# Weights by tiles of 128 columns and one matrix of per-channel vectors in a streaming RWKV-7 / S5 / mLSTM layer

## The chip, the cores and the metric

The kernel runs on one core of one Trainium2 chip. The metric is the device time of one execution in microseconds (us). The engines are PE (matmul; PEld is its weight load), DVE (vector), ACT (scalar), POOL (GpSimd) and SP, whose queue issues most DMA transfers; ACT issues the others. All arithmetic is in float32; the large matmuls run on operands split into a high part, rounded to the matmul's own format, and the remainder.

## The reference

One layer is computed for a prompt of 16 + 2048 tokens and for 64 tokens of a running stream, D = 1024:

```python
proj = (x @ p['w_in']).astype(F32)                       # x: normalised input, w_in: 1024 x 11144
rw_cols, rw_gate, s5_u, s5_gate, ml_qk, ml_v, ml_if, ml_o, ml_z, merge = split_cols(proj, IN_SIZES)
y_rw, ... = rwkv7_branch(rw_cols, rw_gate, ...)          # recurrence with 12 heads of 64
y_s5, ... = s5_branch(s5_u, s5_gate, ...)                # diagonal complex recurrence, then a 512 x 512 GLU
y_ml, ... = mlstm_branch(ml_qk, ml_v, ml_if, ml_o, ml_z, ...)   # 4 heads of 192, chunks
gates = jax.nn.sigmoid(merge + p['b_merge']).reshape(x.shape[:2] + (N_BRANCH, D_MODEL))
merged = (gates[..., 0, :] * (y_rw @ p['w_br_rw']) + gates[..., 1, :] * (y_s5 @ p['w_br_s5'])
          + gates[..., 2, :] * (y_ml @ p['w_br_ml']))
out = merged @ p['w_out']
x_new = layer_norm(DN_ALPHA * x.astype(F32) + out, p['ln_g'], p['ln_b'])
```

It returns x_new for both groups and the states that each branch leaves. There are some twenty per-channel vectors (norm gains and biases, shift weights, conv taps, gate biases, initial states).

## The kernel before

**Blocks.** The 2128 tokens are cut into five blocks (`BLOCKS`, 4 to 7 chunks of 64; block 0 also holds the sample and the meta tokens). Block 0 is loaded and normalised by `ln_first` (L205 to L246), later ones by `ln_stage`, one block ahead. The normalised x, channel on the partition, is held as `xh` and `xl`, eight tiles of 128 channels each.

**Projections.** `proj` (L437) makes 128 output columns of x @ w_in: three products (hi x hi, hi x lo, lo x hi) for each of eight k tiles, 24 matmuls at L434. The weight comes from `load_w` (L416). In block 0, `split_w` (L394) reads the 128 columns from `w_in` in two halves of four k tiles. The view of w_in puts the row within a k tile on the partition, so a half of 128 x 4 x 128 floats (256 KB) consists of 512 pieces of 512 B, each 44.6 KB from the next. ACT casts the half to `whi` (L405), POOL subtracts it to `wlo` (L406), and both are stored to `wsp` in DRAM (L411) in rows of 2 KB. Later blocks load `whi` and `wlo` from there (L425), 512 KB of rows of 2 KB for each half. `wraw` has 3 buffers, `whi` and `wlo` 4 each.

**Order.** Generators for the three branches are interleaved in `mix`; the gate pass (L1502) makes the 24 tiles of the merge gates for a block with its own buffers `ghi`, `glo` and PSUM tag `f`. The framework then schedules all instructions per engine with a model of its own, and each engine and queue runs its list in order. Transfers take eight semaphores in turn, so one waits on its queue until the transfer eight places before it has landed.

**Vectors.** `add_rows` (L265) lists 22 vectors as rows of 128 channels, 294 rows in all. `load_rows` (L294) reads them by 24 transfers on SP (L303) into tiles of 128 rows, PE transposes the tiles (L309) and DVE copies them to `PT` (L310), 128 x 294, so that `pcol` gives a column with the channel on the partition. in_g and in_b are loaded ahead of `ln_first`, the others behind it. `derive` (L315) makes scaled copies on DVE.

**Other weights.** `ml_gates` (L838) reads the 8 columns of the mLSTM's i and f gates as pieces of 32 B, in each of the five blocks. `s5_block` reads `s5_w_glu` at L1416 (4 fetches a block). In `merge_pass`, three passes over tokens fetch w_br_rw, w_br_s5 and w_br_ml in `branch_w` (L1571) and w_out at L1665, all through `split_w` in pieces of 512 B; PE works on them at L1565.

Of the kernel before, what the change touches and what calls it, by code (L numbers as in the profile page):

```python
# [19 lines left out]
KD = D // 128  # L20
# [13 lines left out]
O_RW, O_RG, O_S5U, O_S5G, O_MQ, O_MK, O_MV, O_MIF, O_MO, O_MZ, O_MG = (  # L34
    0, 2432, 3200, 3712, 4224, 4992, 5760, 6528, 6536, 7304, 8072)
# [8 lines left out]
RMAX = 448  # L44
# [39 lines left out]
def tile_trunk(ctx: ExitStack, tc: tile.TileContext, I, O, dbg=None, parts=("rw", "s5", "ml", "mg")):  # L84
    nc = tc.nc
    V, S, G, PE = nc.vector, nc.scalar, nc.gpsimd, nc.tensor
# [6 lines left out]
    wp = ctx.enter_context(tc.tile_pool(name="wp", bufs=1))  # L93
# [20 lines left out]
    def psum(shape, tag):  # L114
        return pt(ps, shape, tag, bufs=PSB[tag])
# [7 lines left out]
    ident = pt(cst, (128, 128), "ident")  # L123
# [138 lines left out]
    rows_spec = []
    col = {}

    def add_rows(name, ap2d):  # L265
        n = ap2d.shape[0]
        col[name] = sum(r[1] for r in rows_spec)
        rows_spec.append((name, n, ap2d))

    def vec(name):  # L270
        return I[name][0].rearrange("(n p) -> n p", p=128)

    add_rows("in_g", I["in_ln_g"].rearrange("(n p) -> n p", p=128))
    add_rows("in_b", I["in_ln_b"].rearrange("(n p) -> n p", p=128))
    add_rows("mu", vec("rw_mu"))
    for nm in ("rw_w0", "rw_a0", "rw_kk", "rw_ka", "rw_ln_g", "rw_ln_b"):
        add_rows(nm, vec(nm))
    add_rows("rk", I["rw_rk"][0].rearrange("(n a) d -> n (a d)", a=2))
    add_rows("shift", I["state_rwkv_shift"][0, 0].rearrange("(n p) -> n p", p=128))
    add_rows("s5_d", vec("s5_d"))  # L280
    add_rows("s5_b_glu", vec("s5_b_glu"))
    add_rows("conv_w", I["ml_conv_w"][0].rearrange("j (n p) -> (j n) p", p=128))
    add_rows("conv_b", vec("ml_conv_b"))
    add_rows("conv_s", I["state_mlstm_conv"][0, 0].rearrange("j (n p) -> (j n) p", p=128))
    add_rows("ml_ln_g", vec("ml_ln_g"))
    add_rows("b_merge", vec("b_merge"))
    for nm in ("s5_a_re", "s5_a_im"):
        add_rows(nm, I[nm][0].rearrange("(q a) p -> q (a p)", a=2))
    for nm in ("state_s5_re", "state_s5_im"):
        add_rows(nm, I[nm][0, 0].rearrange("(q a) p -> q (a p)", a=2))  # L290
    NR = sum(r[1] for r in rows_spec)
    PT = pt(cst, (128, NR), "PT")

    def load_rows(lo, hi, tags):  # L294
        r0, r1 = (col[rows_spec[lo][0]], NR if hi == len(rows_spec) else col[rows_spec[hi][0]])
        rt = [pt(rp, (128, RMAX), tags[i])[:, 0:128] for i in range((r1 - r0 + 127) // 128)]
        r = 0
        for name, n, ap in rows_spec[lo:hi]:
            a = 0
            while a < n:  # L300
                ti, off = divmod(r + a, 128)
                m = min(n - a, 128 - off)
                nc.sync.dma_start(rt[ti][off:off + m, :], ap[a:a + m, :])  # L303
                a += m
            r += n
        for i, t in enumerate(rt):
            m = min(128, r1 - r0 - 128 * i)
            p = psum((128, 128), "tr")
            PE.transpose(p[:, :m], t[:m, :], ident[:m, :m])  # L309
            V.tensor_copy(PT[:, r0 + 128 * i:r0 + 128 * i + m], p[:, :m])  # L310

    def pcol(name, j=0, n=1):
        return PT[:, col[name] + j:col[name] + j + n]
# [3 lines left out]
        V.tensor_scalar(t, pcol(src, 0, n), mul, add, ALU.mult, ALU.add)  # L317
        return t

    load_rows(0, 2, ["rk"])  # L320
    ln_first(blocks[0])
    load_rows(2, len(rows_spec), ["kk", "L", "Bc"])

    ones = pt(c1, (128, 128), "ones")
    V.memset(ones, 1.0)
# [60 lines left out]
                e.dma_start(t.bitcast(F32)[:, :b.T], xT_d[b.i][j, :, k, :])  # L386
                cur[nm].append(t)

    w_in = I["w_in"][0].rearrange("(k p) c -> p k c", p=128)

    WBUF = {"w": (3, 4),
            "g": (2, 2)}
# [23 lines left out]
    def load_w(pool, off, first, tag="w"):  # L416
        nh = WBUF[tag][1]
        if first:
            wh, wl = split_w(pool, w_in[:, :, off:off + 128], KD, 128, tag, keep=off)
            return wh, wl  # L420
        hi, lo = [], []
        for k in range(0, KD, 4):
            for j, (nm, out) in enumerate((("hi", hi), ("lo", lo))):
                t = pt(pool, (128, 4, 128), tag + nm, F32R, bufs=nh)
                nc.sync.dma_start(t.bitcast(F32), wsp_d[off][k // 4, j])  # L425
                out += [t[:, m] for m in range(4)]
        return hi, lo
# [410 lines left out]
    def ml_gates(b):  # L838
        T = b.T
        nch = len(b.tiles)  # L840
        raw = pt(wp, (128, KD, 8), "wraw", bufs=WBUF["w"][0])
        nc.sync.dma_start(raw, w_in[:, :, O_MIF:O_MIF + 8])
        wh, wl = [], []
        for k in range(0, KD, 4):
            h = pt(wp, (128, 4, 128), "whi", F32R, bufs=WBUF["w"][1])
# [468 lines left out]
    def s5_block(b, u_d, y_d):  # L1314
# [82 lines left out]
        for i in range(4):  # L1397
# [11 lines left out]
            V.scalar_tensor_tensor(y, a, 1.0, y, ALU.add, ALU.mult)  # L1409
            Gs.append(y)  # L1410
            yield
        wg = I["s5_w_glu"][0].rearrange("(k p) c -> p k c", p=128)
        for i in range(4):
            ch = slice(128 * i, 128 * i + 128)
            raw = pt(wp, (128, 4, 128), "wraw", bufs=WBUF["w"][0])
            nc.sync.dma_start(raw, wg[:, :, ch])  # L1416
            p = psum((128, 512), "d")
            pv = p[:, :T].rearrange("p (s c) -> p s c", s=8)
            for k in range(4):
                PE.matmul(pv, raw[:, k], Gs[k], start=k == 0, stop=k == 3)  # L1420
# [91 lines left out]
    def merge_pass():  # L1512
# [18 lines left out]
        w_br = {k: I["w_br_" + k][0].rearrange("(k p) c -> p k c", p=128) for k in ("rw", "s5", "ml")}  # L1531
        w_out = I["w_out"][0].rearrange("(k p) c -> p k c", p=128)
        nyk = [0]

        def yk(dt):
# [35 lines left out]
        def branch_w(B, bi, d):  # L1571
            nm, yd, kt = BR[bi]
            th = pt(pool["th"], (128, TB), "th2", bufs=2)
            for b, lo, o, m in seg[B]:
                nc.scalar.dma_start(th[:, o:o + m], g_d[b.i][D * bi + 128 * d:D * bi + 128 * d + 128, lo:lo + m])
            return split_w(wp, w_br[nm][:, :, 128 * d:128 * d + 128], kt, 128) + (th,)

        wnext = branch_w(0, 0, 0)
        ynext = []
# [39 lines left out]
        for B, n_ in enumerate(TBS):  # L1619
# [36 lines left out]
            for grp in ([[slice(0, LG)], [slice(LG, n_)]] if last else [hsl]):  # L1656
                for d in range(8):
                    c0, c1_ = grp[0].start, grp[-1].stop
                    xr = [pt(pool["b"], (128, TB), f"xr{j}", bufs=2) for j in range(2)]
                    for j in range(2):  # L1660
                        for b, lo, o, m in seg[B]:
                            a, e = max(o, c0), min(o + m, c1_)
                            if a < e:
                                nc.scalar.dma_start(xr[j][:, a:e], xT_d[b.i][j, :, d, lo + a - o:lo + e - o])
                    wh, wl = split_w(wp, w_out[:, :, 128 * d:128 * d + 128], KD, 128)  # L1665
                    t = oT[d]
                    for sl in grp:
                        p = psum2((128, sl.stop - sl.start), "g")
# [86 lines left out]
```

## Time and profile before

| | |
|---|---|
| median of 3 runs (lowest, highest) | 4103.11 us (4101.01, 4103.15) |
| profiled execution: its own time, its span | 4099.27 us, 4097.5 us |
| busy share of the span | PE 92%, DVE 62%, ACT 30%, POOL 16% |
| DMA | 837 MB in 814882 packets, 204 GB/s; under 512 B 220262, under 2 KB 574798 packets |
| fetches of 256 KB into wraw | w_in 174, w_out 64, w_br 72 (and 48 of 128 KB), s5_w_glu 20 |

A page of the profile divides the span into 40 slices and gives each a digit, the busy share in tenths. The view by windows gives each engine's busy time in chosen stretches, with PE's granted clock and the busy share of the 16 DMA engines. The share adds up the times of packets, so it can pass 100% in a short stretch. The view of waits tells which engine stood still, and what released it; the chain of waits follows the work that ended last back to its start. Idle time of an engine that nothing waits for costs nothing.

### The profile page before, as it was taken

How to read it: one execution, taken by the hardware profiler on the slowest of the kernel's cores; microseconds unless marked ns; L12 is line 12 of the kernel's file. 1: busy time of each engine (PE TensorE's matmuls, PEld its weight loads, DVE VectorE, ACT ScalarE, POOL GpSimd, SP SyncE). 2: the span in 40 equal slices, each digit the busy share in tenths (PEclk: the TensorE clock that was granted, in tenths of full speed). 3: DMA queues.
4: the chain of work that ended last, by engine and by line, in shares of the span. 5: the costliest groups of instructions: out<-in, count | busy, mean ns of one | idle time of the engine just before them, and what ended most of it. 6: DMA issues, size and time to landing. Idle time of an engine off the chain costs nothing.

```text
span 4097.5 us, 77030 instructions
## 1 busy us (share of the span) xinstructions
PE 3785.1 (92%) x27117; PEld 3302.3 (81%) x27117; DVE 2535.4 (62%) x8332; ACT 1210.1 (30%) x2655; POOL 661.6 (16%) x951
## 2 busy tenths in 40 slices
PE   6886778989999899999999999999999998999997
PEld 5775567878888788888778888878888787999997
DVE  6679875455566556656636656665666554357476
ACT  5443333232222232222322322232323232222222
POOL 5442133200010000001000000000000000232335
PEclk9997798999999999999999999999999999999999
DMA  8995479956676766667675666666575556566555
GB/s 250 287 290 172 124 244 271 299 178 188 185 227 200 240 205 188 206 204 216 201 227 170 210 191 211 205 220 205 175 218 184 167 170 182 170 192 196 157 180 166
DMA packets 814882, 837.19 MB, mean 204 GB/s; under 512 B 220262, under 2 KB 574798, under 8 KB 814494
## 3 DMA queue, kind: packets, MB, share of 16 engines
q1 hardware_dynamic: 736606, 758.96, 60.0%
q10 hardware_dynamic: 77888, 73.28, 6.0%
q8 instruction: 215, 3.52, 0.4%
q14 instruction: 173, 1.42, 0.1%
HBM read 635.89 MB, written 198.18 MB: 204 GB/s over the span
## 4 chain that ended last, share of the span: by engine, by line
PE 63%; DMA 15%; DVE 13%; SPq 3%; issue 2%; ACT 2%; POOL 1%; ACTq 0%; DVEq 0%; POOLq 0%
PE d L434 28%; PE f L434 9%; PE z L1565 7%; PE g L1565 4%; DMA wraw<-in_w_in_dram 2%; PE py L728 1%; PE d L1420 1%; PE tr L581 1%; DMA xT<-X 1%; PE tr L699 1%; PE tr L707 1%; DVE Z L620 1%; DVE Ztmp L618 1%; PE o L1009 1%; DMA Uin<-Ud 1%
## 5 line engine op out<-in xcount | busy, mean ns | idle before, releaser
L434 PE MATMUL d<-xh,whi 128*128 128x448 f32 (+1 forms) x2520 | 946.0, 375 | 47.6 <-ACT whi L405 18.3
L434 PE MATMUL d<-xh,wlo 128*128 128x448 f32 (+1 forms) x2520 | 932.8, 370 | 11.1 <-POOL wlo L406 10.8
L434 PE MATMUL d<-xl,whi 128*128 128x448 f32 (+1 forms) x2520 | 928.4, 368 | 0.0
L434 PEld LDWEIGHTS d<-xh,whi 128*128 128x128 f32 x2520 | 485.6, 193 | 106.6 <-ACT whi L405 21.8
L434 PEld LDWEIGHTS d<-xh,wlo 128*128 128x128 f32 x2520 | 485.2, 193 | 60.5 <-POOL wlo L406 16.1
L434 PEld LDWEIGHTS d<-xl,whi 128*128 128x128 f32 x2520 | 485.9, 193 | 39.6 <-issue 7.0
L406 POOL TENSOR_TENSOR wlo<-wraw,whi 128x512 fp32r<-128x512 f32 (+1 forms) x310 | 397.3, 1291 | 566.3 <-ACT whi L405 534.0
L434 PE MATMUL f<-xh,ghi 128*128 128x448 f32 (+1 forms) x912 | 348.1, 382 | 46.9 <-ACT gt L1509 26.9
L434 PE MATMUL f<-xh,glo 128*128 128x448 f32 (+1 forms) x912 | 342.5, 376 | 9.0 <-DMA glo<-wsp 6.5
L434 PE MATMUL f<-xl,ghi 128*128 128x448 f32 (+1 forms) x912 | 335.4, 368 | 0.0
L405 ACT CAST whi<-wraw 128x512 fp32r<-128x512 f32 (+1 forms) x310 | 180.1, 586 | 459.8 <-PE z L1565 95.9
L618 DVE TENSOR_TENSOR Ztmp<-Uin,Z 128x60 f32<-128x60 f32 (+24 forms) x930 | 206.1, 222 | 103.2 <-DMA Uin<-Ud 90.3
L434 PEld LDWEIGHTS f<-xh,ghi 128*128 128x128 f32 x912 | 178.3, 196 | 72.4 <-ACT gt L1509 33.6
L620 DVE TENSOR_TENSOR Z<-Z,Ztmp 128x60 f32<-128x60 f32 (+24 forms) x930 | 211.0, 227 | 13.6
L434 PEld LDWEIGHTS f<-xh,glo 128*128 128x128 f32 x912 | 178.1, 195 | 29.2 <-DMA glo<-wsp 10.8
L1565 PE MATMUL z<-ya,whi 128*128 128x384 f32 (+1 forms) x784 | 191.6, 324 | 0.6 <-DVE th L1637 0.6
L434 PEld LDWEIGHTS f<-xl,ghi 128*128 128x128 f32 x912 | 178.6, 196 | 12.4 <-issue 1.6
L946 DVE SCALAR_TENSOR_TENSOR X<-X,PT 128x448 f32<-128x448 f32 (+1 forms) x180 | 122.4, 680 | 46.3 <-ACT X L944 42.7
L1565 PEld LDWEIGHTS z<-ya,whi 128*128 128x128 f32 x784 | 137.5, 188 | 1.5 <-DVE th L1637 0.6
L1565 PE MATMUL z<-ya,wlo 128*128 128x384 f32 (+1 forms) x384 | 124.3, 324 | 0.0
L1509 ACT ACTIVATE gt<-f,hbm 128x448 f32<-128x448 f32 (+1 forms) x114 | 69.8, 613 | 181.1 <-PE f L434 150.3
L1565 PE MATMUL z<-yb,whi 128*128 128x288 f32 (+1 forms) x512 | 120.7, 318 | 2.0 <-DVE th L1637 1.8
(732 smaller groups left out, 6863.7 us busy)
## 6 DMA issues: line engine op xcount, KB each, us to landing
whi<-wsp SPq DMA_DIRECT2D x504, 256.0 KB
wlo<-wsp SPq DMA_DIRECT2D x504, 256.0 KB
ghi<-wsp SPq DMA_DIRECT2D x192, 256.0 KB
glo<-wsp SPq DMA_DIRECT2D x192, 256.0 KB
wraw<-in_w_in_dram SPq DMA_DIRECT2D x174, 256.0 KB
wsp<-whi SPq DMA_DIRECT2D x126, 256.0 KB
wsp<-wlo SPq DMA_DIRECT2D x126, 256.0 KB
gt<-gt SPq DMA_DIRECT2D x96, 224.0 KB
```

Source lines behind the costliest of these rows:

```text
L405: S.copy(h[:, :n, :M], raw[:, :n, :M])
L406: G.tensor_tensor(l[:, :n, :M], raw[:, :n, :M], h.bitcast(F32)[:, :n, :M], ALU.subtract)
L434: PE.matmul(p, a[k], c, start=i == 0, stop=i == 3 * KD - 1)
L581: i = PE.matmul(p[h][:, c].rearrange("p (j t) -> p j t", j=2), bk[h][:, c0 + c, :], AQ[hs[h], c0 + c], start=True, stop=True)
L618: V.tensor_tensor(t3, Uin[:, j:j + 1, j + 1:32].to_broadcast((128, m, n)), Z[:, 0:m, j:j + 1].to_broadcast((128, m, n)), ALU.mult)
L620: V.tensor_tensor(Z[:, 0:m, j + 1:32], Z[:, 0:m, j + 1:32], t3, ALU.add)
L699: PE.matmul(p[hs[h], c], Tt[hs[h], c0 + c, :], AR[hs[h], c0 + c], start=True, stop=True)
L707: PE.matmul(p[hs[h], c], PX[hs[h], c0 + c, 0, :], AT[hs[h], c0 + c, h, :], start=True, stop=True)
L728: i = PE.matmul(o, a, x, start=start, stop=stop, skip_group_check=True)
L946: V.scalar_tensor_tensor(acc[:, :w], raw[:, j:j + w], pcol("conv_w", 12 * j + ti), acc[:, :w], ALU.mult, ALU.add)
L1509: S.activation(t[:, :T], p[:, :T], AF.Tanh, scale=0.5, bias=hbm[:, j:j + 1])
L1565: PE.matmul(p, a[k], c[:, sl], start=i == 0, stop=i == n - 1)
```

## The change

Before the kernel is built, `kernel` now lays the inputs out anew with `_layout`: w_in as 87 tiles of 128 columns, each with the row within a k tile first, then the k tile, then the column (`w_tiles`), so that a half tile is 128 pieces of 2 KB; the 8 gate columns apart (`w_if`, 256 B for each partition); the other five weights as tiles in the same way; and the 294 rows of vectors as one matrix of 128 x 294 (`pt`). On the core, `PT` is loaded by one transfer, and `add_rows`, `load_rows`, their transposes and copies are gone. What is computed from weights and vectors, and from which buffers, stays the same.

```diff
-    def load_rows(lo, hi, tags):
...
-                nc.sync.dma_start(rt[ti][off:off + m, :], ap[a:a + m, :])
...
-            PE.transpose(p[:, :m], t[:m, :], ident[:m, :m])
-            V.tensor_copy(PT[:, r0 + 128 * i:r0 + 128 * i + m], p[:, :m])
+    nc.sync.dma_start(PT, I["pt"])
...
-    load_rows(0, 2, ["rk"])
     ln_first(blocks[0])
-    load_rows(2, len(rows_spec), ["kk", "L", "Bc"])
...
-    w_in = I["w_in"][0].rearrange("(k p) c -> p k c", p=128)
+    def w_tile(off):
+        return I["w_tiles"][(off if off < O_MIF else off - 8) // 128]
...
-            wh, wl = split_w(pool, w_in[:, :, off:off + 128], KD, 128, tag, keep=off)
+            wh, wl = split_w(pool, w_tile(off), KD, 128, tag, keep=off)
...
-        nc.sync.dma_start(raw, w_in[:, :, O_MIF:O_MIF + 8])
+        nc.sync.dma_start(raw, I["w_if"])
...
-            nc.sync.dma_start(raw, wg[:, :, ch])
+            nc.sync.dma_start(raw, I["s5_w_glu"][i])
...
-            return split_w(wp, w_br[nm][:, :, 128 * d:128 * d + 128], kt, 128) + (th,)
+            return split_w(wp, I["w_br_" + nm][d], kt, 128) + (th,)
...
-                    wh, wl = split_w(wp, w_out[:, :, 128 * d:128 * d + 128], KD, 128)
+                    wh, wl = split_w(wp, I["w_out"][d], KD, 128)
...
+def _tiles(w):
+    k, c = w.shape
+    return w.reshape(k // 128, 128, c // 128, 128).transpose(2, 1, 0, 3)
```

The change moves instructions. On SP's queue, before, the last row loads (`L` and `Bc` are tiles for rows, `bif` and `msam` small vectors of the mLSTM) stand just ahead of the first fetches of w_in:

```order
L303 DMA L_335<-in_s_a_im_dram 16x128
L303 DMA L_335<-in_state_s_re_dram 10x128
L303 DMA Bc_336<-in_state_s_re_dram 6x128
L303 DMA Bc_336<-in_state_s_im_dram 16x128
L823 DMA bif_424<-in_ml_b_if_dram 4x1
L824 DMA bif_424<-in_ml_b_if_dram 4x1
L826 DMA msam_427<-in_state_mlstm_m_dram 4x1
L404 DMA wraw_465<-in_w_in_dram 128x4x128
L404 DMA wraw_473<-in_w_in_dram 128x4x128
```

They are transfers 24 to 33 of the queue. On SP's queue of the changed kernel, from its first transfer on (`va`, `AT` and `X` are the tiles that x is loaded into):

```order
L267 DMA PT_111<-in_pt_dram 128x294
L214 DMA va_115<-in_x_sample_dram 64x1024
L214 DMA AT_121<-in_meta_dram 16x1024
L214 DMA AT_127<-in_x_prompt_dram 128x1024
L214 DMA X_133<-in_x_prompt_dram 128x1024
L779 DMA bif_385<-in_ml_b_if_dram 4x1
L780 DMA bif_385<-in_ml_b_if_dram 4x1
L782 DMA msam_388<-in_state_mlstm_m_dram 4x1
L360 DMA wraw_426<-in_w_tiles_dram 128x512
L360 DMA wraw_434<-in_w_tiles_dram 128x512
```

The first fetch of w_in is now the ninth transfer and was the thirty-second. On ACT, before, the program begins with the scaling of x (L232) and its casts to `xh` (L241), and the first casts of weights (L405) stand among the latter:

```order
L232 ACTIVATE va_120<-va_120,nb_43_160,rs_40_146 64x1024
L232 ACTIVATE AT_126<-AT_126,nb_43_160,rs_40_146 16x1024
L232 ACTIVATE AT_132<-AT_132,nb_43_160,rs_40_146 128x1024
L232 ACTIVATE X_138<-X_138,nb_43_160,rs_40_146 128x1024
L241 ACTIVATE xh_44_162<-d_179,PT_111 128x64
L241 ACTIVATE xh_48_166<-o_196,PT_111 128x64
L241 ACTIVATE xh_44_162<-d_214,PT_111 128x16
L241 ACTIVATE xh_48_166<-o_231,PT_111 128x16
L405 CAST whi_463<-wraw_465 128x512
```

On ACT of the changed kernel (L361 is the cast of weights, L808 and L809 those of the gate columns):

```order
L361 CAST whi_424<-wraw_426 128x512
L361 CAST whi_432<-wraw_434 128x512
L808 CAST whi_484<-wraw_482 128x4x4 x2
L808 CAST whi_494<-wraw_482 128x4x4 x2
L809 CAST wlo_485<-wraw_482 128x4x4 x2
L809 CAST wlo_495<-wraw_482 128x4x4 x2
L232 ACTIVATE va_115<-va_115,nb_41_155,rs_38_141 64x1024
L232 ACTIVATE AT_121<-AT_121,nb_41_155,rs_38_141 16x1024
```

The casts of the first weights have moved ahead of the scaling of x.

## Rows read from the trace of the kernel before

**Rows 1.** The page: the span, and the DMA share in 40 slices.

```profile
span 4097.5 us, 77030 instructions
...
DMA  8995479956676766667675666666575556566555
```

**Rows 2.** Windows by stage: start:end, length, busy us (instructions) by engine, PE's clock, DMA share, GB/s.

```profile
core 0: us, PE busy (x) PEld busy (x) DVE busy (x) ACT busy (x) POOL busy (x), PEclk, DMA share, GB/s
0.00:50.00 50.00, 24.58 (x119) 22.22 (x119) 30.51 (x117) 28.19 (x65) 27.26 (x73) 0.97 0.73 221
50.00:300.00 250.00, 210.30 (x1495) 189.15 (x1493) 170.17 (x472) 105.53 (x236) 120.86 (x144) 0.94 0.94 288
300.00:600.00 300.00, 215.61 (x1598) 174.68 (x1597) 262.05 (x1164) 104.07 (x283) 82.36 (x122) 0.81 0.58 177
600.00:800.00 200.00, 171.19 (x1377) 149.86 (x1376) 105.70 (x408) 63.01 (x146) 59.02 (x54) 0.90 0.96 288
800.00:3400.00 2600.00, 2510.93 (x18429) 2134.31 (x18430) 1571.80 (x5415) 735.18 (x1629) 144.88 (x378) 0.99 0.64 200
3500.00:4050.00 550.00, 540.69 (x3324) 535.21 (x3323) 315.32 (x548) 136.01 (x224) 206.10 (x166) 1.00 0.60 178
```

**Rows 3.** Windows of instructions that read or write wraw (ACT: the casts).

```profile
50.00:300.00 250.00, 0.00 (x0) 0.00 (x0) 0.00 (x0) 48.65 (x79) 103.20 (x79) 0.94 0.94 288
300.00:600.00 300.00, 0.00 (x0) 0.00 (x0) 0.00 (x0) 29.23 (x48) 62.41 (x47) 0.81 0.58 177
600.00:800.00 200.00, 0.00 (x0) 0.00 (x0) 0.00 (x0) 25.63 (x42) 55.29 (x42) 0.90 0.96 288
```

**Rows 4.** The chain of waits by line, 50 to 300 us, then 600 to 800 us.

```profile
by line: DMA wraw<-in_w_in_dram 16.5%; PE d L434 12.7%; issue 5.9%; DVE Z L620 5.9%; DVE Ztmp L618 4.6%; POOL wlo L406 3.7%; SPq L411 3.7%; ACT whi L405 3.1%; DMA xT<-X 2.9%; DMA Uin<-Ud 2.6%; DVE BK L560 2.0%; DMA wsp<-whi 2.0%; DVE X L946
...
by line: PE f L434 22.7%; DMA wsp<-ghi 12.6%; DMA s5wo<-Kd 7.6%; DMA wraw<-in_w_in_dram 6.5%; PE d L434 5.9%; issue 3.5%; DMA w<-s5wo 2.7%; DMA xl<-xT 2.7%; DVE sB L1356 2.4%; DMA s5wo<-sB 2.4%; ACT gt L1509 2.2%; DMA wraw<-in_s_w_glu_dram 
```

**Rows 5.** DMA in 46.5:49.5, 2085:2089, 882:886: packets by size; queue, packets, MB, share.

```profile
DMA packets 1938, 0.97 MB, mean 323 GB/s; under 512 B 45, under 2 KB 1938, under 8 KB 1938
q1 hardware_dynamic: 1938, 0.97, 113.0%
...
DMA packets 762, 1.38 MB, mean 345 GB/s; under 512 B 88, under 2 KB 88, under 8 KB 762
q1 hardware_dynamic: 762, 1.38, 99.5%
...
DMA packets 674, 1.22 MB, mean 304 GB/s; under 512 B 74, under 2 KB 124, under 8 KB 674
q1 hardware_dynamic: 674, 1.22, 103.4%
```

**Rows 6.** Issues on SP by tile: ns minimum/median/maximum, first and last start in us.

```profile
L404 SPq DMA_DIRECT2D wraw<-in_w_in_dram x174: 383/448/1769, 15.8 to 758.7; - x174
...
L411 SPq DMA_DIRECT2D wsp<-whi x126: 319/377/1920, 20.4 to 570.0; - x126
```

**Rows 7.** The timeline of the first 30 us: start us, us, engine, line, operation [idle before].

```profile
3.81 0.29 SPq L303 DMA_DIRECT2D kk<-in_rw_mu_dram  x1
...
14.20 1.24 ACT L232 ACTIVATE va<-va,nb,rs 64x1024 f32<-64x1024 f32 x1 [7.51 <-DVE nb L225]
...
14.45 0.32 SPq L303 DMA_DIRECT2D Bc<-in_state_s_im_dram  x1
...
15.84 0.95 SPq L404 DMA_DIRECT2D wraw<-in_w_in_dram  x2
...
21.07 1.27 POOL L406 TENSOR_TENSOR wlo<-wraw,whi 128x512 fp32r<-128x512 f32 x1
...
29.37 0.65 PE L434 MATMUL d<-xh,whi 128*128 128x336 f32 x1 [0.80 <-DVE AT L242]
```

**Rows 8.** Waits from 50 to 300 us: us in total, times, longest.

```profile
ACT whi L405 <- DMA wraw<-in_w_in_dram: 34.1, 25, 4.2
...
PE d L434 <- ACT whi L405: 15.7, 7, 6.0
...
PE d L434 <- POOL wlo L406: 8.3, 11, 3.4
```

More of the change, by code (lines that the diff above doesn't have):

```diff
@@ L260, in rsqrt @@
                 V.scalar_tensor_tensor(out, a, 1.5, out, ALU.add, ALU.mult)
[L262 to L291, printed above, removed]
-    PT = pt(cst, (128, NR), "PT")
-    def load_rows(lo, hi, tags):
[L295 to L302, printed above, removed]
-                nc.sync.dma_start(rt[ti][off:off + m, :], ap[a:a + m, :])
[L304 to L308, printed above, removed]
-            PE.transpose(p[:, :m], t[:m, :], ident[:m, :m])
-            V.tensor_copy(PT[:, r0 + 128 * i:r0 + 128 * i + m], p[:, :m])
+    col, NR = {}, 0
@@ L312, in pcol @@
+    for name, n in _ROWS:
+        col[name] = NR
+        NR += n
+    PT = pt(cst, (128, NR), "PT")
+    nc.sync.dma_start(PT, I["pt"])
     def pcol(name, j=0, n=1):
@@ L1411, in s5_block @@
             yield
-        wg = I["s5_w_glu"][0].rearrange("(k p) c -> p k c", p=128)
         for i in range(4):
@@ L1530, in merge_pass @@
         pool["th"] = pool["e"] = pR.enter_context(tc.tile_pool(name="mxe", bufs=1, side=RS, reuse_waits="tile"))
-        w_br = {k: I["w_br_" + k][0].rearrange("(k p) c -> p k c", p=128) for k in ("rw", "s5", "ml")}
-        w_out = I["w_out"][0].rearrange("(k p) c -> p k c", p=128)
         nyk = [0]
@@ L1732, with _layout @@
 _OUTS = [((1, 2048, 1024), 'float32'), ((1, 64, 1024), 'float32')] + [(s, 'float32') for s in _ST + _ST]
+_ROWS = (("in_g", 8), ("in_b", 8), ("mu", 19), ("rw_w0", 6), ("rw_a0", 6), ("rw_kk", 6), ("rw_ka", 6),
+         ("rw_ln_g", 6), ("rw_ln_b", 6), ("rk", 6), ("shift", 19), ("s5_d", 4), ("s5_b_glu", 4), ("conv_w", 48),
+         ("conv_b", 12), ("conv_s", 36), ("ml_ln_g", 6), ("b_merge", 24), ("s5_a_re", 16), ("s5_a_im", 16),
+         ("state_s5_re", 16), ("state_s5_im", 16))
+_SRC = {"in_g": "in_ln_g", "in_b": "in_ln_b", "mu": "rw_mu", "rk": "rw_rk", "shift": "state_rwkv_shift",
+        "conv_w": "ml_conv_w", "conv_b": "ml_conv_b", "conv_s": "state_mlstm_conv"}
+def _tiles(w):
+    k, c = w.shape
+    return w.reshape(k // 128, 128, c // 128, 128).transpose(2, 1, 0, 3)
+def _layout(inputs):
+    import numpy as np
+    a = {n: np.asarray(inputs[n]) for n in _INS}
+    w = a.pop("w_in")[0]
+    a["w_tiles"] = np.concatenate([_tiles(w[:, :O_MIF]), _tiles(w[:, O_MIF + 8:])])
+    a["w_if"] = w[:, O_MIF:O_MIF + 8].reshape(KD, 128, 8).transpose(1, 0, 2)
+    for n in ("s5_w_glu", "w_br_rw", "w_br_s5", "w_br_ml", "w_out"):
+        a[n] = _tiles(a[n][0])
+    rows = []
+    for name, n in _ROWS:
+        v = a.pop(_SRC.get(name, name)) if name not in ("s5_a_re", "s5_a_im") else a.pop(name)
+        rows.append(v.reshape(n, 128))
+    a["pt"] = np.concatenate(rows).T
+    return {n: np.ascontiguousarray(v) for n, v in a.items()}
 def kernel(**inputs):
@@ L1743 @@
     arrays, ins, outs = {}, {}, []
-    for name in _INS:
-        a = _np.ascontiguousarray(inputs[name])
+    for name, a in _layout(inputs).items():
         arrays[f"in_{name}_dram"] = a
```

## Prediction

> **What bounds the kernel now.** I read the page first, for the span and the DMA strip: the span is 4097.5 us, and DMA is dense only in the first eight of the 40 slices (digits 8, 9, 9, 5, 4, 7, 9, 9), then mostly 5 to 7 [rows 1]. So I cut the span there and asked for the windows by stage [rows 2]. Five stages come out. From 0 to 50 us block 0 is loaded and normalised; PE is busy 24.58 of 50 us. From 50 to 300 us the projections of block 0 run: the DMA engines are busy 0.94 of the time, PE 210 of 250 us, DVE 170. From 300 to 600 us DVE is the full one (262 of 300) and DMA only 0.58. From 600 to 800 us the gate pass of block 0 runs: DMA 0.96, PE 171 of 200, DVE 106. After that PE is the bound: 2511 of 2600 us busy up to 3400, and 541 of 550 in the merge pass.
>
> The reader should take from this that the two stages full of DMA are exactly those in which the weights are fetched from w_in: the casts that read wraw are counted by stage in [rows 3], 79, 48 and 42 of them, one for each fetch of 256 KB. Each fetch also brings two 256 KB stores (hi and lo) to wsp in 2 KB rows, which the change leaves alone. The chain of waits agrees: of the 250 us from 50 to 300, 16.5% (41 us) is the landing of wraw, the largest single entry, and of the 200 us from 600 to 800 it is 6.5% (13 us) [rows 4].
>
> **Part 1: 512-byte rows become 2 KB rows.** A fetch of 256 KB has 512 packets of 512 B now and 128 of 2 KB afterwards. The price comes from two short windows in which one size fills the engines [rows 5]. Around 48 us, 1938 packets, practically all of 512 B, took 113.0% of 16 engines in 3 us: 1.13 x 16 x 3.0 / 1938 = 28.0 ns each, so 512 of them over 16 engines are 0.90 us. Around 2087 us, of 762 packets 674 are of 2 KB or more: 0.995 x 16 x 4.0 / 674 = 94.5 ns when the 88 small ones are charged to them, so 128 are 0.76 us. A fetch thus saves 0.14 us of the 16 engines. The bounds: with the small packets counted as equals the 2 KB packet is 83.6 ns and the saving 0.23 us; in the window at 884 us (103.4%, 550 packets of 2 KB or more) it is at most 120 ns, a fetch 0.96 us, and the saving is slightly negative. I take 0.14, since the window at 2087 us is the purer one and is full, as the stages in question are.
>
> The Trainium skill speaks against this part: its page "DMA: Bandwidth & Descriptors", section "Specifications", puts the smallest transfer for line rate at 512 B. By that rule the rows of now are at line rate already, 0.14 becomes 0 and only part 3 is left of the sum; the window at 884 us bears it out, that at 2087 us does not.
>
> Where the DMA engines end last, that saving goes straight to the time: 79 fetches from 50 to 300 us x 0.14 = 11.1 us, and 42 from 600 to 800 us x 0.14 = 5.9 us. From 300 to 600 us DVE covers the fetches (262 of 300 us busy), so of 48 x 0.14 = 6.7 us I count a third, 2.2 us. A check from the other side: if only the chain's own share of wraw shrinks, by 0.14 of 0.90, it is 16% of 41 and 13 us, 8 us in place of 17. The truth may lie between; I keep the first number because the stores to wsp queue behind the same engines and are late by the same amount. The issue on SP gets a little shorter as well: 448 ns median for a w_in fetch against 377 ns for a store with 2 KB rows [rows 6], 0.07 us x 174 = 12 us of a queue that is held most of the time by waits of the stores for ACT and POOL; I count nothing for it, and it is covered by those waits. If they shrink, it is worth up to a few us.
>
> **Part 2: s5_w_glu, w_br and w_out in the same layout.** The saving per fetch is the same, but PE is busy 541 of 550 us in the merge pass with the clock at 1.00 and DMA at 0.60 [rows 2], so I count nothing; the cover is PE's own matmuls, and without it the 184 fetches of the pass, 48 of them of half the size, would show 160 x 0.14 = 22 us. The 20 fetches of s5_w_glu lie in stages that PE bounds: nothing.
>
> **Part 3: one matrix PT for 24 row loads.** SP issues 22 of these one after the other from 3.81 to 14.77 us (the last is 0.32 us from 14.45), and the first fetch of w_in is issued at 15.84 us [rows 7]. Afterwards it is SP's ninth transfer, and an issue takes 0.3 to 0.5 us [rows 7], so it goes out at about 5 us, 11 us earlier. What of it is on the path is less. The first matmul of a projection, at 29.37 us, comes behind the normalisation: ACT scales from 14.20 us on, released by DVE's nb, and then transposes and casts follow [rows 7]. The x tiles land no earlier (PT itself, 150 KB, now runs ahead of them). But four transposes on PE, four copies out of PSUM and the derived vectors leave DVE's stretch before nb (some 1 us), and the two casts of wraw and the small casts of the gate weights move ahead of the scaling on ACT, out of the stretch between it and the first matmul; POOL loses two subtractions of 1.27 us there [rows 7]. I count 3 us, between 0 (all of it beside other work) and 8 (all of it on the path). The wait that stands next is PE's for the casts of x. A risk of the sign against: the small loads of the S5 setup now stand on SP ahead of the stores of x; SP was waiting for ACT there anyway, so nothing.
>
> **Part 4: the order elsewhere.** Scheduling is done anew, and rows of the same kind are exchanged on all engines up to the last block; the merge pass keeps its order on PE. No instruction is added. I count 0 and keep 5 us either way for the range.
>
> **Sum.** 3 + 11.1 + 5.9 + 2.2 = 22 us. The profiled execution took 4099.3 us in all, so 4077 us; the median of the three runs is 3.8 us above the profiled one, 4103.1, so I forecast **4080 us**, the 4081 of the sum rounded down for the SP queue.
>
> **Rivals.**
> *A, a fetch costs its bytes.* Then rows of any length take 0.9 us, and only the start is shorter: 4103 - 3 = 4100 us, no change that can be told. For it speaks the window at 884 us [rows 5], and that the wait ahead of PE from 50 to 300 us is put down to the cast and the subtraction (15.7 and 8.3 us) rather than to DMA [rows 8]; against it, that ACT in turn waits 34.1 us for wraw in the same stretch [rows 8], and the two full windows. It is the mechanism of the skill's rule above. Chance 0.15.
> *B, slower by the new order.* PE stands still for only 89 us from 800 to 3400 us [rows 2], because tiles of the gate pass fill the waits of the recurrences. These tiles are the ones that change place most. If they are used up early and later waits stand open, PE idles. Half as much idle time again is 45 us and makes 4103 - 22 + 45 = 4126 us; it decides for slower from 30 us on (22 gained and 8 of the bound). Against it: the number of tiles is the same and each block's tiles stay in the same stretch. Chance 0.07.
> *C, more than forecast.* The saving is 0.23 us, counted on all 169 fetches of block 0, and the start gives 3: 42 us, 4061 us. For it speaks that the stages are queues, in which a fetch waits for the stores before it. Chance 0.12.
>
> **How the numbers follow.** The forecast has 0.66. A measurement of this kernel can tell about 0.2%, 8 us, from no change, so faster means under 4095 us: forecast and C, 0.78; the same is A, 0.15; slower is B, 0.07. The range leaves out B and the outer parts of A and C: from 4055 (a little beyond C) to 4102 us (A, with 2 us for part 4).
>
> **What would show it.** Right: the packets under 2 KB fall by about 180,000 (330 fetches of 512 packets, 48 of 256 and five of 1024, less what stays shorter than 2 KB); from 50 to 300 us the DMA share falls below 0.94, or the stage gets shorter at the same share; the last fetch of w_in is issued about 20 us before the 758.7 us of now [rows 6]; the first projection matmul begins at 25 to 27 us; PE's idle time from 800 us on stays near 89 us in 2600. Wrong: the 2 KB fetch takes 0.9 us of the engines as before (A); the fetches get cheaper and block 0 ends at the same time, so that POOL, ACT or DVE was the bound there; or the time is lost after 800 us (B).

## The result, and the profile after

The changed kernel is slower: 4135.68 us median (4122.55 to 4145.61, 9 runs) against 4108.27 us (4101.01 to 4120.34, 9 runs) of the kernel before in the same sessions, ratio 1.0065, 95% interval 1.0050 to 1.0079. That is about 27 us, where 22 us less were forecast, and it lies outside the range. Later sessions ran on chips on which the kernel before took 4121 to 4124 us; so only ratios are compared below, and 0.0010 of a ratio is 4.1 us.

The page of the changed kernel, its span, busy times and packets:

```profile
span 4133.9 us, 77001 instructions
...
PE 3814.3 (92%) x27113; PEld 3321.3 (80%) x27113; DVE 2538.3 (61%) x8328; ACT 1210.6 (29%) x2655; POOL 661.9 (16%) x951
...
DMA packets 677195, 837.18 MB, mean 203 GB/s; under 512 B 215606, under 2 KB 394872, under 8 KB 676808
```

The busy times on the page of the kernel before:

```profile
PE 3785.1 (92%) x27117; PEld 3302.3 (81%) x27117; DVE 2535.4 (62%) x8332; ACT 1210.1 (30%) x2655; POOL 661.6 (16%) x951
```

Windows of the changed kernel by stage, with the columns of [rows 2]:

```profile
0.00:50.00 50.00, 22.03 (x109) 21.14 (x110) 30.07 (x112) 27.56 (x64) 27.11 (x73) 0.97 0.74 227
50.00:300.00 250.00, 212.62 (x1485) 192.03 (x1484) 166.34 (x468) 106.23 (x236) 122.66 (x144) 0.92 0.87 284
300.00:600.00 300.00, 213.23 (x1546) 171.26 (x1545) 264.57 (x1157) 100.96 (x279) 81.58 (x120) 0.80 0.53 171
600.00:800.00 200.00, 170.93 (x1451) 147.94 (x1450) 107.44 (x405) 62.91 (x148) 61.02 (x57) 0.91 0.91 282
800.00:3400.00 2600.00, 2511.02 (x18235) 2130.25 (x18234) 1550.03 (x5297) 727.44 (x1598) 142.97 (x378) 0.98 0.64 199
```

Three things are to be seen. The packets under 2 KB fell by 574798 - 394872 = 179,926, and the DMA share fell from 0.94 to 0.87 and from 0.96 to 0.91 in the two stages of the fetches [rows 2]: the transfers did get cheaper. Yet by 800 us PE has got through 4591 matmuls, against 4589 before [rows 2]: nothing was gained there. And from 800 to 3400 us PE stands still for 89 us, as before, but gets through 18235 matmuls in place of 18429 [rows 2]: 194 less, 1.1% of 2600 us or 27 us. Over the whole program PE is busy for 3814.3 us in place of 3785.1, with the same matmuls but for the four transposes of the row loads: 29 of the 36 us by which these two traces differ. Most of the time was lost while PE was busy.

Two more rows, of the fetches of w_in on SP (tile view) and of the first projection matmul (timeline):

```profile
L360 SPq DMA_DIRECT2D wraw<-in_w_tiles_dram x174: 328/445/2478, 4.5 to 778.1; - x174
```

```profile
31.40 0.65 PE L390 MATMUL d<-xh,whi 128*128 128x336 f32 x1 [2.25 <-DVE AT L242]
```

The first fetch goes out at 4.5 us, 11 us earlier than in [rows 6]; the last at 778.1 us, 19 us later. The first projection matmul, at 29.37 us in [rows 7], begins 2.0 us later.

### The profile page after: what moved, and what is told of

Its sections match the earlier page's. It is cut to its first block, busy times and chain, and to the rows that moved or that the text cites. A ratio compares the mean times of both kernels' runs of the same rounds, so it can differ in the third digit from the quotient of the medians.

```text
span 4133.9 us, 77001 instructions
## 1 busy us (share of the span) xinstructions
PE 3814.3 (92%) x27113; PEld 3321.3 (80%) x27113; DVE 2538.3 (61%) x8328; ACT 1210.6 (29%) x2655; POOL 661.9 (16%) x951
## 2 busy tenths in 40 slices
DMA packets 677195, 837.18 MB, mean 203 GB/s; under 512 B 215606, under 2 KB 394872, under 8 KB 676808
## 4 chain that ended last, share of the span: by engine, by line
PE 62%; DMA 15%; DVE 14%; SPq 2%; ACT 2%; issue 2%; POOL 1%; ACTq 0%; DVEq 0%; POOLq 0%
PE d L390 27%; PE f L390 8%; PE z L1518 7%; PE g L1518 4%; DMA xT<-X 2%; DMA ghi<-wsp 2%; PE py L684 1%; PE d L1375 1%; PE tr L537 1%; DVE Ztmp L574 1%; DMA E<-rd 1%; PE tr L655 1%; DMA X<-in_x_prompt_dram 1%; DVE Z L576 1%; PE tr L663 1%
## 5 line engine op out<-in xcount | busy, mean ns | idle before, releaser
L361 ACT CAST whi<-wraw 128x512 fp32r<-128x512 f32 (+1 forms) x310 | 179.6, 586 | 458.0 <-PE z L1518 99.2
L576 DVE TENSOR_TENSOR Z<-Z,Ztmp 128x60 f32<-128x60 f32 (+24 forms) x930 | 205.8, 221 | 14.3
```

Of the source, the lines that this page charges most:

```text
L361: S.copy(h[:, :n, :M], raw[:, :n, :M])
L576: V.tensor_tensor(Z[:, 0:m, j + 1:32], Z[:, 0:m, j + 1:32], t3, ALU.add)
```

## The experiments

**The means.** An instruction that both kernels have stands at the same place of the program text. So the order in which each engine issues can be recorded from one kernel and laid down in another: for each engine, every instruction is given an edge of order to the one before it in the record. The edge adds no wait and no semaphore.

```diff
     with _tile.TileContext(nc, schedule_with_timeline_sim=True) as tc:
         tile_trunk(tc, ins, outs)
+        _pin(nc, tc, _mybir)
...
+        for a, b in zip(idx[:-1], idx[1:]):
+            a, b = real[int(a)], real[int(b)]
...
+            tc.add_manual_dep(
+                b, a.name,
+                mybir.DependencyInfo(mybir.DependencyClass.NoSync, mybir.DependencyReason.DATA),
+                reason="recorded order")
```

The theories were O, that the new order costs the time, and L, that the layouts themselves do.

### Layout and order apart

**full_order_before**: the changed kernel, in the order of the kernel before.

> The whole change, but every engine issues its instructions in the order of the kernel before (the recorded order is laid down as an order edge from each instruction to the next on its engine; the 24 row loads, their four transposes and four copies drop out of it and the load of PT stands where the first of them stood). Theory O (the time is lost by the new instruction order, the layouts themselves cost nothing): 4085 to 4110 us, that is the kernel before (4108) or up to 22 us less; the last fetch of w_in issued before 758.7 us, and PE idle near 89 us from 800 to 3400 us. Theory L (the 2 KB rows or the early PT load themselves cost the time): about 4135 us as the changed kernel, whatever the order.

Measured: ratio 0.9988 (0.9975 to 1.0001). PE is idle for 89 us from 800 to 3400 us, as expected; the last fetch of w_in is issued at 772.1 us, though, and not before 758.7.

**oldrows_order_after**: the weights as before, PT and the order as after.

```diff
-            wh, wl = split_w(pool, w_tile(off), KD, 128, tag, keep=off)
+            wh, wl = split_w(pool, w_in[:, :, off:off + 128], KD, 128, tag, keep=off)
```

> The kernel after with all weights in their old layout (rows of 512 B), PT as one load, every engine in the recorded order of the kernel after. Theory O: the loss stays, 4130 to 4155 us (the changed kernel's 4136, plus up to 20 if the short rows cost what I forecast). Theory L: without the 2 KB rows the loss is gone, about 4105 us.

Measured: 1.0063 (1.0048 to 1.0079), as the changed kernel. So laying an order down costs nothing that can be told either.

**w2k_order_before**: the kernel before with the weights' new layout alone, its order kept.

```diff
-            wh, wl = split_w(pool, w_in[:, :, off:off + 128], KD, 128, tag, keep=off)
+            wh, wl = split_w(pool, w_tile(off), KD, 128, tag, keep=off)
```

> The kernel before with only the weights in the new layout (2 KB rows), row loads as before, every engine in the recorded order of the kernel before: nothing but the rows' length differs. Theory O: 4088 to 4108 us, 19 us less if part 1 of the prediction holds, the same if a fetch costs its bytes. Theory L: 4120 to 4135 us.

Measured: 0.9993 (0.9979 to 1.0006).

**w2k_free_order**: the same without `_pin`.

> The same kernel with its order made by the scheduler anew. The instructions are those of the run above, so whatever differs from it is the order's alone. Theory O: it differs from the run above by more than 8 us, either way (4090 to 4140 us). Theory L: it equals the run above within 8 us.

Measured: 1.0026 (1.0009 to 1.0042).

Theory L falls. In either order the length of the rows makes 0.0007 or less; the order makes 1.0065 - 0.9988 = 0.0077, 32 us. A third order, made for the weights alone, costs 14 us more than that of before. All that the change itself brings is about 5 us (0 to 10).

**half_fetch**: what a fetch is worth in the order of before.

```diff
-            nc.sync.dma_start(raw[:, :n, :M], src[:, k:k + n])
-            S.copy(h[:, :n, :M], raw[:, :n, :M])
...
+                nc.sync.dma_start(raw[:, :2, :M], src[:, k:k + 2])
+                rr = raw[:, None, :2, :M].to_broadcast((128, 2, 2, M))
+                S.copy(h[:, :n, :M].rearrange("p (r m) c -> p r m c", r=2), rr)
...
```

> The whole change in the order of the kernel before, with each fetch of w_in brought down to one half: two of its four rows per partition are fetched and used twice, so 128 KB and half the packets for each of the 174 fetches of block 0; half of w_in is left out of what is computed. Number, length and order of the instructions stay. If the DMA engines bound the stages from 50 to 300 and from 600 to 800 us (my part 1), half a fetch of 0.76 us is 0.38 us, and 79 and 42 of them give 30 and 16 us: ratio about 0.987 to 0.990. If the engines were not the bound and only latency and the other engines count: 0.996 to 1.000, with the DMA share from 50 to 300 us near 0.75.

Measured: 0.9944 (0.9926 to 0.9962), 0.0044 or 18 us (9 to 27) less than full_order_before, between the two theories. The stage from 50 to 300 us, first in full_order_before, then in half_fetch:

```profile
50.00:300.00 250.00, 211.45 (x1478) 189.64 (x1477) 168.33 (x467) 103.91 (x234) 120.27 (x143) 0.92 0.88 285
```

```profile
50.00:300.00 250.00, 212.48 (x1509) 192.10 (x1507) 173.33 (x476) 104.80 (x235) 123.58 (x146) 0.93 0.78 249
```

The share of the engines falls about as reckoned (0.94, 0.88, 0.78), but of the 46 us of their time that half a fetch was reckoned to take away in the two stages, 18 reach the kernel's time, about 0.4. The chain of waits from 50 to 300 us tells what ends last instead, first in full_order_before, then in half_fetch:

```profile
by line: DMA wraw<-in_w_tiles_dram 15.7%; PE d L390 13.6%; DVE Z L576 8.2%; DVE Ztmp L574 6.1%; issue 4.5%; SPq L367 3.2%; DVE BK L516 2.9%; ACT whi L361 2.6%; DVE X L902 2.1%; SPq L592 1.9%; POOL wlo L362 1.8%; DMA ys<-sB 1.5%; DMA Uin<-Ud
```

```profile
by line: PE d L397 24.6%; DVE Z L583 6.5%; DMA wsp<-whi 6.2%; DVE Ztmp L581 4.6%; issue 3.0%; DMA wraw<-in_w_tiles_dram 2.4%; DVE X L909 2.3%; DVE BK L523 1.9%; SPq L374 1.8%; POOL wlo L364 1.8%; PE tr L544 1.7%; DMA Uin<-Ud 1.5%; DMA wsp<-
```

The landing of wraw shrinks from 39 us of the chain to 6, and PE's own projection matmuls (`d`) grow from 34 us to 61: the chain now runs through them. From before to full_order_before, the 2 KB rows took the landing of wraw only from 16.5% [rows 4] to 15.7%, 2 us of the chain.

### Where the order loses

Three mixtures of the two orders, cut at points of the program up to which both have issued nearly the same instructions:

> The whole change; every engine issues in the recorded order of the kernel after up to about 870 us of the program (the end of block 0 and of its gate pass), and in the order of the kernel before from there on. The order as a whole is worth 0.77% (1.0065 against 0.9988 of the kernel before), some 32 us. If it is lost in block 0, where the gate tiles wait for their casts: ratio about 1.005 to 1.007. If it is lost in later blocks: 0.997 to 1.000. If it is spread over the program: about 1.001.

> The same, with the order of the kernel after only from about 870 to 2200 us, where the trace of after falls behind that of the whole change in the order of before by 4 us at 1400, 15 at 1500 and 33 at 2000, and comes back to 16 at 2100. If the loss is made there: ratio 1.003 to 1.007. If that is only another order of the same work: 0.997 to 1.000. Spread: about 1.001.

> The same, with the order of the kernel after only from about 2200 us to the end. By the traces (16 us at 2100, 19 at the end) little is lost here: 0.998 to 1.001. Spread: about 1.001. Over 1.003 would say that the shift between two single traces doesn't tell where an order loses.

Measured: 1.0004 (0.9989 to 1.0019), 1.0044 (1.0027 to 1.0062) and 1.0007 (0.9993 to 1.0021). Against 0.9988 the middle holds 0.0056, 23 us; the first and the last part 7 and 8 us, at the edge of what can be told. The three add up to 0.0091, the whole order to 0.0077; with the uncertainty of each that is the same. In the middle, the timelines of PE show this. `py` is the output of `rw_back`, the closing products of the RWKV recurrence: pairs of matmuls of 64 columns, with weights of 128x64 or 64x64, at L728 before and L684 after; `d` is a projection, `tr` and `o` are other small products. The kernel before:

```profile
1515.30 0.36 PE L434 MATMUL d<-xh,whi 128*128 128x448 f32 x1
1515.50 0.37 PE L434 MATMUL d<-xl,whi 128*128 128x448 f32 x1
1515.80 0.56 PE L728 MATMUL py<-XV,AT 128*64 128x64 f32 x10
1516.29 0.94 PE L581 MATMUL tr<-AQ,BK 64*128 64x128 f32 x12
1517.15 0.80 PE L728 MATMUL py<-XV,AT 128*64 128x64 f32 x18
1517.88 0.33 PE L728 MATMUL py<-Scar,AQ 64*64 64x64 f32 x4
1518.05 0.87 PE L728 MATMUL py<-Hw,AQ 64*64 64x64 f32 x24
1518.84 0.47 PE L434 MATMUL d<-xh,wlo 128*128 128x448 f32 x1
```

and the kernel after:

```profile
1516.11 0.33 PE L684 MATMUL py<-Hw,AQ 64*64 64x64 f32 x2
1516.37 0.47 PE L390 MATMUL d<-xl,whi 128*128 128x448 f32 x1
1516.77 0.32 PE L684 MATMUL py<-Hw,AQ 64*64 64x64 f32 x2
1517.03 0.47 PE L390 MATMUL d<-xh,wlo 128*128 128x448 f32 x1
...
1522.03 0.47 PE L684 MATMUL py<-Hw,AQ 64*64 64x64 f32 x2
1522.44 0.74 PE L390 MATMUL d<-xh,wlo 128*128 128x448 f32 x1
1523.11 0.47 PE L684 MATMUL py<-Hw,AQ 64*64 64x64 f32 x2
...
1528.02 0.57 PE L390 MATMUL d<-xh,whi 128*128 128x448 f32 x1
1528.39 0.57 PE L390 MATMUL d<-xl,whi 128*128 128x448 f32 x1
...
1532.38 0.37 PE L390 MATMUL d<-xh,whi 128*128 128x448 f32 x1
```

Read the starts. Before, 28 pairs stand in groups, and the last 12 take 0.79 us, 0.066 us each. After, the scheduler has put them one by one between projection matmuls: pair and matmul together take 0.66 us from start to start (1516.11 to 1516.77), where a matmul among its like takes 0.21 and a pair in a group 0.07 to 0.08. Each step to the small weights and back thus costs some 0.37 us, and none of it shows as idle.

The timeline of before also has a pair of `py` with as many columns, but with weights of 128x128, alone between projection matmuls:

```profile
1505.87 0.33 PE L728 MATMUL py<-Hw,PB 128*128 128x64 f32 x2
1506.01 0.45 PE L434 MATMUL d<-xl,whi 128*128 128x448 f32 x1
1506.30 0.36 PE L434 MATMUL d<-xh,wlo 128*128 128x448 f32 x1
```

There pair and matmul take 0.43 us (1505.87 to 1506.30). So 0.23 of the 0.66 us goes with the small weights, not with the number of columns.

From 1518.5 to 1532 us all is slower still in the kernel after. The windows, first of after, then of before over the same pairs:

```profile
1504.00:1518.00 14.00, 14.00 (x70) 8.27 (x70) 10.45 (x35) 3.98 (x9) 0.48 (x3) 1.00 0.29 89
1518.00:1532.00 14.00, 14.00 (x41) 9.37 (x41) 6.41 (x15) 1.64 (x3) 1.55 (x1) 0.52 0.15 44
```

```profile
1515.00:1529.00 14.00, 14.00 (x130) 12.74 (x129) 7.10 (x31) 3.43 (x9) 0.24 (x1) 1.00 0.55 166
```

The granted clock falls to 0.52, the level of 1.2 GHz, without an idle gap ahead of it: what PE did before the fall is the alternation. This is no accident of one trace. From 1500 to 1560 us the clock is 0.89 to 0.94 in the five traces with these pairs one by one (after, oldrows_order_after, mix_middle, and below mix_1420 and spread_before), and 1.00 in all thirteen others. PE is "busy" 14 of 14 us everywhere, with 130 matmuls before against 70 and 41 after. The Trainium skill, page "TensorEngine Tiling (Array Packing)", section "Key Properties", says that a change of the tiling mode drains TensorE; it gives no price. The rows agree in that the steps are dear; that a step to the small weights is such a change, no row shows. The Trainium skill's page "Perfetto Trace Analysis", section "Identifying the Most-Contended Engine", holds that the matmuls' busy share is a poor measure of how near a kernel is to its roofline (the most that the engine could do) and that of the weight loads (PEld) a good one. The trace agrees: here PEld falls from 12.74 of 14 us to 8.27 and 9.37.

### The pairs, moved by hand

In **bunch_after** and **spread_before** only PE's list is changed, in 65 and in 45 neighbouring places of its 21378; the lists of all other engines stay. **mix_1420** and **mix_1610** are two more mixtures. The kernels hold the order packed, so bunch_after's change is given as a sketch (`s` is PE's list, `seg` the stretch):

```python
    e["PE"] = s[:lo] + [i for i in seg if not is_py(i)] + [i for i in seg if is_py(i)] + s[hi:]
```

> The kernel after in its own order, but for one stretch of TensorE's list, near 1510 to 1530 us of its program: there 28 readout pairs of the tile py (128x64 and 64x64) stand one by one between projection matmuls. They are moved together behind the 38 other matmuls of the stretch, nothing else moves. Theory S (a change between a projection matmul and such a pair costs TensorE about 0.39 us, since the pair and the matmul behind it take 0.66 us from start to start in the trace, against 0.21 for the matmul and 0.07 for a pair among others): about 20 changes less, 8 to 11 us less than after, ratio 1.004 to 1.0045, and the segment between about 1420 and 1610 us shorter by as much (195 us now). Rival (the segment is longer for other reasons, its DMA waits or the gate tiles that left it): 1.006 to 1.007 as after.

> The opposite: the whole change in the order of the kernel before, where 28 such pairs stand in one group near 1525 us. The last 20 of them are put one by one behind the projection matmuls that follow; nothing else moves. Theory S: 20 x 0.39 = 8 us more than in the order of before (0.9988), ratio about 1.0007, and the segment between about 1420 and 1605 us, 184.4 us in that order, grows to about 192. Rival: 0.998 to 0.9995 and 184 to 186 us.

> The whole change in the order of the kernel before, with the order of after only between about 1420 and 1610 us, the segment in which the traces in the order of after are 11 to 15 us longer (195 to 200 us) than those in the order of before (184 to 186). If the loss of the middle part (0.0056, 23 us) comes from there: ratio 1.0015 to 1.0025, segment 195 to 200 us. If a segment's length in the trace tells nothing (what is lost there comes back later): 0.998 to 1.000.

> The same with the order of after only between about 1610 and 2200 us, the rest of the middle part. It should hold what the run above leaves of the 23 us: 8 to 12 us, ratio 1.001 to 1.0015, if the loss can be added up by segments; 0.998 to 0.9995 if it is all in the segment before.

Measured: bunch_after 1.0027 (1.0010 to 1.0044), spread_before 1.0021 (1.0005 to 1.0037), mix_1420 1.0047 (1.0030 to 1.0064), mix_1610 1.0020 (1.0006 to 1.0033).

In place of the segments by number of instructions, a cleaner measure is the time between two instructions that every kernel has: on DVE the first product of `sB` and `PT` into `sA` in a block's S5 output, and on PE the first `py<-Scar,PB` of the block behind it. Before, after, bunch_after and spread_before, in the timelines of DVE and PE:

```profile
1423.60 0.69 DVE L1404 SCALAR_TENSOR_TENSOR sA<-sB,PT,sA 128x448 f32<-128x448 f32 x1 [12.72 <-DMA sB<-u]
1587.99 0.43 PE L728 MATMUL py<-Scar,PB 128*128 128x64 f32 x2
```

```profile
1436.68 0.68 DVE L1360 SCALAR_TENSOR_TENSOR sA<-sB,PT,sA 128x448 f32<-128x448 f32 x1 [11.33 <-DMA sB<-u]
1615.41 0.43 PE L684 MATMUL py<-Scar,PB 128*128 128x64 f32 x2
```

```profile
1428.98 0.68 DVE L1360 SCALAR_TENSOR_TENSOR sA<-sB,PT,sA 128x448 f32<-128x448 f32 x1 [11.37 <-DMA y<-sB]
1592.13 0.43 PE L684 MATMUL py<-Scar,PB 128*128 128x64 f32 x2
```

```profile
1434.98 0.69 DVE L1360 SCALAR_TENSOR_TENSOR sA<-sB,PT,sA 128x448 f32<-128x448 f32 x1 [12.26 <-DMA y<-sB]
1618.34 0.43 PE L684 MATMUL py<-Scar,PB 128*128 128x64 f32 x2
```

Between the two marks it is 164.4 us before, 178.7 after, 163.2 with the pairs bunched in the order of after, and 183.4 with 20 of them spread in the order of before. Other traces bear it out: 163.8 to 165.5 us in the seven others that have the order of before here, 174.5 in mix_1420, 179.7 in oldrows_order_after and 180.8 in mix_middle. In the timeline of bunch_after 14, 2 and 12 pairs again take 0.97, 0.16 and some 0.8 us in a row:

```profile
1503.99 1.03 PE L684 MATMUL py<-XV,AT 128*64 128x64 f32 x28
1504.96 0.33 PE L684 MATMUL py<-Scar,AQ 64*64 64x64 f32 x4
1505.12 0.87 PE L684 MATMUL py<-Hw,AQ 64*64 64x64 f32 x24
```

The windows over the pairs, first of bunch_after, then of spread_before:

```profile
1503.00:1517.00 14.00, 14.00 (x123) 12.10 (x122) 12.79 (x34) 2.17 (x4) 1.90 (x3) 1.00 0.53 176
```

```profile
1529.00:1545.00 16.00, 16.00 (x72) 9.38 (x73) 1.00 (x2) 0.00 (x0) 0.24 (x1) 0.77 0.35 99
```

So 28 pairs that are moved by some 10 us give back 0.0038, 16 us, and 20 that are moved the other way cost 0.0033, 14 us. Theory S holds both ways. It undersized its price: 8 to 11 us were expected, since I had left out the clock. By the timeline of after, 21 single matmuls stand between pairs of this stretch. 13 are at full clock and 8 at the low one, where pair and matmul take 1.07 us (1522.03 to 1523.11). They make 13 x 0.37 + 8 x 0.79 = 11.1 us, and 13 matmuls behind them at 0.37 instead of 0.21 another 2.1: together 13.2 of the 14.3 us by which after is longer than before between the two marks.

mix_1420 holds the whole loss of the middle part (0.0059 above 0.9988), more than was expected. mix_1610 was to hold what is left of it and shows 0.0032, which is too much: two segments' losses, each uncertain by 0.002, don't add up cleanly.

### The rest, and a better version

Half of the order's loss, 0.0039, was left. Other places in which single projection or gate matmuls stand between small ones were taken next. In PE's whole list there are 132 such matmuls in the order of after and 92 in that of before; 22 and none of them stand between two pairs of `py`. Again only PE's list is changed, here as a sketch for **bunch_all_after**. **bunch_all_before** and **seg_bunch_all** do the same to other orders, and **seg_bunched** is one more mixture:

```python
    for a, b in places:
        seg = s[a:b + 1]
        s[a:b + 1] = [i for i in seg if is_big(i)] + [i for i in seg if not is_big(i)]
```

> bunch_after (the kernel after with its 28 pairs together; 1.0027), and in 13 more places of TensorE's list, where single projection matmuls alternate with small ones (54 matmuls, tiles o and tr), the projection matmuls of the place are put ahead of the small ones. If these changes cost 0.2 to 0.3 us each as well, 11 to 16 us less: ratio 0.999 to 1.000, as the order of before. If the rest of the loss is of another kind (waits for inputs): 1.002 to 1.003, or more where the small ones are waited for.

> The whole change in the order of the kernel before, and in the 18 places of TensorE's list where single projection matmuls (59 of them) alternate with small ones the projection matmuls are put ahead of the small ones. If each change costs 0.2 to 0.3 us: 12 to 18 us less than 0.9988, ratio 0.9945 to 0.996, faster than both kernels. If the small ones are waited for, or if only the pairs of 64 columns are dear: 0.998 to 1.000.

> The whole change in the order of the kernel before, with the bunched order of after between about 1420 and 1610 us, where the trace of bunch_after took 180.0 us against 184.4. If that carries over: ratio 0.9975 to 0.998, segment 180 us; as the order of before otherwise (0.9988).

> seg_bunched with its remaining alternations (52 single projection matmuls) bunched as well. If both gains add up: 0.994 to 0.9955; if only the pairs count: 0.9975 to 0.999.

Measured: bunch_all_after 1.0000 (0.9987 to 1.0013), bunch_all_before 0.9979 (0.9968 to 0.9991), seg_bunched 1.0010 (0.9992 to 1.0028), seg_bunch_all 1.0008 (0.9993 to 1.0023).

With nothing but small matmuls moved behind big ones on PE, the changed kernel comes from 1.0065 to 1.0000 in its own order: 27 us, 84% of what the two orders differ by. What is left against 0.9988 can't be told from nothing. In the order of before the same edit brings only 0.0009, less than expected and within the uncertainty. 33 of its 59 single matmuls stand between products of 128x128 weights, and there a matmul and two small ones take 0.42 us in the trace of before (1519.40 to 1519.82), against 0.66 with the small weights; so they have less to give:

```profile
1519.40 0.45 PE L434 MATMUL d<-xh,whi 128*128 128x448 f32 x1
1519.68 0.38 PE L1004 MATMUL o<-t,t 128*128 128x128 f32 x2
1519.82 0.45 PE L434 MATMUL d<-xl,whi 128*128 128x448 f32 x1
```

That this is why is not shown, and the places taken in the order of after are hardly different: about half of them stand between such products there too (27 of 58 by the trace). Why the one edit brought 0.0027 and the other 0.0009 stays open; the uncertainty of each is about 0.002.

seg_bunched is mix_1420 with the 28 pairs together and nothing else moved. So it is a third trial of the pairs: 1.0047 falls to 1.0010, by 0.0037, 15 us. It was expected at 0.9975 to 0.998, and what it keeps above 0.9988, 0.0022 or 9 us, is another loss of that segment's order, at the edge of what can be told and not explained. Bunching on top of it (seg_bunch_all) brought nothing.

bunch_all_before is the fastest version that leaves nothing out: its interval lies below the kernel before, and it is some 0.85% below the changed kernel (0.9979 / 1.0065).

## Why the prediction was wrong

**Part 4 is the step that failed.** "No instruction is added. I count 0 and keep 5 us either way": the new order cost 32 us. Rival B had the sign and the cause, an order made anew, but not the mechanism. It looked for idle time of PE, and that stayed at 89 us, as the prediction's own sign for "right" had it. The loss sits in what PE does while busy: small-weight matmuls put one by one between projection matmuls, and the lower clock behind them. The timeline of before held at least the 0.21, 0.07 and 0.42 us, and the order of after, known in advance, showed 132 such places against 92 and all 22 between two pairs of `py`; I had looked at which tiles change place and not at what stands next to what.

**Part 1 was right in the engines and wrong in the time.** The packets fell as counted and the DMA share fell by 0.06 to 0.07 of 250 us, 15 to 18 us where 11.1 were reckoned for the stage. With the order of after held, oldrows_order_after has, at 282 GB/s as the changed kernel:

```profile
600.00:800.00 200.00, 170.06 (x1451) 146.02 (x1451) 106.48 (x405) 62.91 (x147) 61.41 (x57) 0.90 0.95 282
```

That is 0.95 against 0.91, 8 us of the engines for 42 fetches or 0.19 each: the price of 0.14 was about right. But "that saving goes straight to the time" failed: with the order held, the 2 KB rows are worth 0.0007, 3 us (9 less to 2 more), in place of 19. half_fetch gives the rate, 0.4 of the engines' time; the check from the chain of waits in the prediction, 8 us in place of 17, was the better number. A share of 0.94 with PE at 210 of 250 us is not a stage that DMA alone bounds: by the chain in half_fetch, PE's projection matmuls take the place of most of what the fetches give up.

Rival A gave the better time with the order held, though not for its reason, since the share shows that long rows are cheaper for the engines; its time was right by luck. The rule of the Trainium skill that stood beside it (page "DMA: Bandwidth & Descriptors", section "Specifications", line rate from 512 B on) does not agree with that fall of the share.

**Part 2** held: the first fetch of w_br_s is issued 37.6 us later than before (3561.2 against 3523.6), the span is 36.4 us longer, so the merge pass lost and gained nothing worth telling.

**Part 3** half held. PT is one load and the fetch goes out 11 us earlier, as forecast, but the first projection matmul begins at 31.40 us, not at 25 to 27. The scaling of x begins at 16.96 instead of 14.20 us [rows 7]. The early casts on ACT are not why: ACT is done with them and waits 2.06 us for DVE's nb, an operand of the scaling. DVE makes nb later, since its new order puts small operations of the S5 setup ahead, one of which waits for a transfer:

```profile
13.09 1.54 DVE L1092 COPY sA<-sA 16x128 f32<-16x128 f32 x1 [0.47 <-DMA sA<-in_s_log_dt_dram]
```

```profile
16.96 1.24 ACT L232 ACTIVATE va<-va,nb,rs 64x1024 f32<-64x1024 f32 x1 [2.06 <-DVE nb L225]
```

The prediction saw the small loads of the S5 setup move up on SP and priced them at nothing; it did not look at the operations on DVE that come with them. In the order of before (full_order_before) that matmul begins at 28.98 us, 0.4 earlier than in the kernel before. So 0.4 us was there to be had in place of 3. As a ratio, PT as one load makes 0.0005, from 0.9993 (w2k_order_before) to 0.9988: nothing that can be told.

Rival C, more than forecast, did not happen: with the order held, the whole change brings 5 us (0 to 10), not 42.

## What to carry to other kernels

Where a scheduler makes the order, an edit that only changes a layout can draw a new one; so hold the order fixed to learn what the edit is worth, and price the order by itself. Read what stands next to what on TensorE's list: here small-weight matmuls that alternate one by one with big ones cost several times what they cost in a group, and the busy share of PE did not show it, while the number of matmuls in a window and the weight loads' busy time did. And look at what stands close behind the transfers before counting their saving as time: here, with PE busy for 210 of 250 us, about 0.4 of it came through.

## What was not expected of the hardware

- A step from 128x448 projection matmuls to a pair of 64 columns with 128x64 or 64x64 weights and back takes 0.66 us in all, against 0.21 + 0.07 us in groups. With a pair of 64 columns and 128x128 weights it takes 0.43.
- TensorE's granted clock went to 0.52 for 14 us with no idle gap ahead of it, behind 14 us in which PE was busy throughout but with its weight loads at 8.27 of 14 us; with the same pairs in groups it stayed at 1.00 (bunch_after).
- 28 pairs of matmuls, moved within some 20 us of a program of 4100, change its time by 0.4%.
